# A float32r transformer trunk on one core: its on-chip pools laid out anew

## The chip, the cores and the metric

The kernel runs on one core of a Trainium2 chip. The metric is the device time of one execution in microseconds (us). Engines: PE (TensorE) multiplies matrices, DVE (VectorE), ACT (ScalarE) and POOL (GpSimd) work elementwise, SP (SyncE) issues the DMA transfers. SBUF is the on-chip memory of 128 partitions; an address here is a number of bytes within a partition. PSUM is the memory into which PE accumulates, in banks of 2 KiB a partition.

## The reference

Two layers, each of three blocks with a norm before and after, on x of 256 tokens by 1024:

```python
x = x + 0.5 * rms(swiglu(rms(x, g0), w_in[l,0], w_out[l,0]), g1)     # 1024 -> 2 x 2816 -> 1024
x = x + rms(mixer(rms(x, g2)), g3)
x = x + 0.5 * rms(swiglu(rms(x, g4), w_in[l,1], w_out[l,1]), g5)
```

`swiglu(h)` is `(silu(gate) * up) @ w_out` with `gate, up = split(h @ w_in)`. The mixer projects to 3080 columns: a differential attention of 4 heads (rotary embedding, two softmaxes, their difference on the values, a norm), and an mLSTM of 4 heads (a causal convolution of length 4 over queries and keys, exponential gates, a state carried over chunks of 64 tokens, an output gate). Both outputs, side by side, go through a matrix of 1024 by 1024. All is float32.

## The kernel before

Every product with a weight matrix is made of three float32r passes. An operand is split into hi and lo = value - hi, and `mm3` (L329 to L332) adds hi*hi (L330), hi*lo (L331) and lo*hi (L332) in one PSUM bank. The transposed activations are the stationary operand (128 x 128), the weights the moving one (128 x 512). There are 1312 such triples.

The tokens form two tiles of 128. The weights come as 164 pieces of 1 MiB in the order of use. SP loads a piece into one of three buffers `wr`. Each of its two halves is split by ACT, which writes hi into `wh` (L280), and by DVE, which writes lo into `wl` (L282); both are 4 KiB a partition. `wh` and `wl` have seven buffers each. The pool `k4` has six buffers that a mixer uses for its large tiles (`xpad`, `conv`, `gt`, `ex`, two of `qkT`, `vd`). While `lend` is set, which is everywhere but in the body of a mixer, each half whose running number ends in 2, 5 or 8 goes to two of these:

```python
if self.lend and self.halves % 10 in (2, 5, 8):
    lo = self.k4.tile([P, 1024], F32R, tag="k4", name=f"wl_{i}_{j}")
    hi = self.k4.tile([P, 1024], F32R, tag="k4", name=f"wh_{i}_{j}")
```

All buffers of a tag are as wide as its widest tile, padded to 32 bytes.

An FFN works through 11 chunks of 256 hidden columns. A chunk takes two pieces for its input products (PSUM tag `pin`, stationary tiles `th`, `tl` of the pool `tr`) and one for its output products (tag `bk`, stationary `hh`, `hl` of the pool `hp`). Between them stand silu on ACT, the product on DVE, two transposes per token tile (L461) and the split of the hidden layer into `hh` (L464) and `hl` (L465). The output products of a chunk run one or two chunks late; the last ones of the first token tile and then of the second end the FFN. The first chunk of the first FFN writes to `bk`.

A mixer's input projection runs as steps of one triple each (`part_step`), and its other stages are traced between them at positions given by hand (`AT`); the output projection has stationary tiles `yh`, `yl`, from the pool `tr` too, and the tag `bk`. `conv_input` takes `xpad` out of k4 and clears its first three columns on POOL (L788); ACT fills the rest (L795), ACT and DVE read it (L803, L806).

A planner with a simulated timeline sets the order on each engine from the traced order and the buffers that are free, apart from stretches where PE's order is that of the program text. Pools lie in SBUF in the order in which they are opened, from address 16512 on (a scratch ring of 16 KiB and small constants come first): `const`, `wr`, `wl`, `wh`, `tr`, `k2`, `k4`, `ded`, `hp`, `sm`.

Of the kernel before, what the change touches and what calls it, by code (L numbers as in the profile page):

```python
"""Two layers of macaron FFN / (diff attention | mLSTM) mixer / macaron FFN on one core.

Every product with a weight matrix runs as three float32r passes: an operand is
split exactly into hi (float32r, 12 significant bits) and lo = value - hi, and
hi*hi + hi*lo + lo*hi accumulate in one PSUM bank. The activations (transposed,
128 tokens a tile) are stationary and the weights move, 512 columns at a time.
"""
# [8 lines left out]
F32 = mybir.dt.float32  # L16
# [20 lines left out]
WARM = 6  # L37
PIECES_FFN = 3 * NC_FF
# [11 lines left out]
def _pack(inp):  # L50
    """Lays the inputs out for the kernel, in the order in which it uses them."""
# [67 lines left out]
class _Trunk:  # L119
# [49 lines left out]
    def constants_mix(self):  # L169
# [26 lines left out]
        # lambda of both layers, on every partition  # L196
# [8 lines left out]
        # persistent tiles with fixed parts  # L205
# [22 lines left out]
        nc.gpsimd.memset(self.vx, 1.0)  # L228

# [1 line left out]
    def after(self, ins, others):  # L231
        """ins takes its turn on its engine behind the others."""
        for o in others:
            self.tc.add_manual_dep(ins.ins, o.ins.name, mybir.DependencyInfo(
                mybir.DependencyClass.NoSync, mybir.DependencyReason.DATA), reason="turn")

    def table(self, name, last=None):
        """Loads a set of ScalarE's functions behind everything that uses another set."""
        self.loaded = self.nc.scalar.preload_act_table_set(name)
        self.after(self.loaded, self.users + ([last] if last else []))  # L240
        self.users = []

    def func(self, *args, **kw):
        """An activation that needs the set loaded last."""
        i = self.nc.scalar.activation(*args, **kw)  # L245
        self.after(i, [self.loaded])
        self.users.append(i)
        return i

    def piece(self):  # L250
        """The next 1 MiB of the weights as hi and lo: two times [P, 1024] each. While no
        mixer needs them, its 4 KiB buffers hold some of these."""
        parts = self.begin_piece()
        return [parts(), parts()]

    def begin_piece(self):
        """A function that gives a piece's halves one after the other."""
        nc, i = self.nc, self.piece_at
        self.piece_at += 1
        step = 1024  # L260
        if i in self.early:
            raw, step = self.early[i], 512
        else:
            raw = self.raw_tile(i)
            self.load = nc.sync.dma_start(raw.rearrange("p a b -> p (a b)"), self.a["w"][i])
        js = iter(range(2))

        def part():
            j = next(js)
# [3 lines that stand above are left out]
            else:  # L273
                lo = self.wl.tile([P, 1024], F32R, tag="wl", name=f"wl_{i}_{j}")
                hi = self.wh.tile([P, 1024], F32R, tag="wh", name=f"wh_{i}_{j}")
            self.halves += 1
            turns = self.turns.pop(0) if self.turns else ()
            for c in range(0, 1024, step):
                cs = slice(c, c + step)
                ia = nc.scalar.activation(hi[:, cs], raw[:, j, cs], AF.Copy)  # L280
                self.cast = ia
                iv = nc.vector.tensor_tensor(lo[:, cs], raw[:, j, cs], hi[:, cs].bitcast(F32), op=ALU.subtract)  # L282
                for oa, ov in turns:
                    self.after(ia, [oa] if oa else [])
                    self.after(iv, [ov] if ov else [])
            return hi, lo

        return part
# [4 lines left out]
    def start(self):  # L293
        """The first loads, in the order in which the products need them."""
# [20 lines left out]
    def warm(self, n):  # L315
        """The tensor engine's clock rises while it waits for the first loads."""
        bank = self.bank_bk()
        for _ in range(n):
            self.nc.tensor.matmul(bank, self.zero[:, 0:P], self.zero, start=True, stop=True)

    @staticmethod
    def cols(piece, k):
        """Columns k*512..k*512+511 of a piece, hi and lo."""
# [11 lines left out]
    def rsqrt(self, ss, width=1):  # L335
        """ss -> ss ** -0.5 on [P, width]."""
# [4 lines left out]
    def prenorm(self, t, gi):  # L341
        """Transposed x * gain of token tile t as hi/lo."""
        return [self.prenorm_half(t, gi, hf) for hf in range(2)]
# [19 lines left out]
    def square(self, t, hf, ss):  # L363
        """The mean square of half of token tile t."""
# [3 lines left out]
    def rstd(self, t):  # L368
        """rsqrt(mean(x ** 2) + eps) of token tile t."""
# [5 lines left out]
    def rsqrt_sum(self, ss, eps):  # L375
        """(ss0 + ss1 + eps) ** -0.5"""
# [9 lines left out]
    def postnorm(self, t, po, g, half):  # L386
        """x += (0.5 if half else 1) * rmsnorm(po) * g."""
# [83 lines left out]
    def ffn(self, pre, gi_post):  # L471
# [16 lines left out]
        if not xT:  # L488
            # the first phase: both token tiles from the start
# [41 lines left out]
        else:  # L531
            # the first two chunks: the first token tile runs ahead of the second
# [46 lines left out]
        # the last chunks: all of the first token tile, then the second  # L579
# [15 lines left out]
    def mixer(self, pre, gi_post):  # L595
# [19 lines left out]
        # output projection  # L615
# [24 lines left out]
    def lambdas(self):  # L640
        """-(exp(q1.k1) - exp(q2.k2) + lambda_init) of both layers, on every partition."""
# [8 lines left out]
class _Mixer:  # L650
    """The stages of one layer's mixer, in the order in which they are traced."""
# [13 lines left out]
    def traverse(self, tr, pin, ws, pins1, ws1, load_gpost):  # L665
        """The rest of the input projection in steps of three matrix products, with everything
        else that the mixer does between them."""
# [53 lines left out]
    def stages(self):  # L721
        """(step, stage): the stage takes its turn once so many steps of the products are traced."""
# [37 lines left out]
    def part(self, t, kh, pin, w):  # L760
        """Half the contraction of one token tile with one group of 512 columns."""
# [7 lines left out]
    def transposed(self, a, tag="ptr"):  # L769
        """The four 128-column blocks of a, transposed, in a PSUM bank."""  # L770
# [12 lines left out]
    # ---- queries and keys of the mLSTM  # L783
    def conv_input(self, t, pin):
        tr = self.tr
        if t == 0:
            self.xpad = tr.t4("xpad", (P, 4, S + 3))
            tr.nc.gpsimd.memset(self.xpad[:, :, 0:3], 0.0)  # L788
# [26 lines left out]
    # ---- gates of the mLSTM  # L815
# [13 lines left out]
    def gate_inputs(self):  # L829
        """log i and the forget gate's input, tokens on partitions."""  # L830
# [24 lines left out]
    def gate_rows(self):  # L855
        """Cumulative log forget gates b, u = log i - b and the running maxima, heads on
        partitions 0..3, 32..35, 64..67 and 96..99."""
# [34 lines left out]
    def gate_exps(self, t):  # L892
        """exp(u_s - M_j) within a chunk and s <= j, zero elsewhere: one contraction over both."""
# [9 lines left out]
    def gate_decays(self):  # L903
        """The decays, input weights and exp(-m)."""
# [8 lines left out]
        # the first chunk's state is zero: its queries meet it with a factor of zero  # L913
# [5 lines left out]
    def weighted_qk(self):  # L919
        """Queries times their decay, keys times their input weight."""  # L920
# [24 lines left out]
    def intra_weights(self):  # L945
        """exp(u_s - M_j) * (k_s . q_j) / 8. Heads on other partitions use another PSUM bank."""
# [13 lines left out]
    # ---- attention  # L960
# [15 lines left out]
    def roped(self, i, t, scale):  # L976
        """Queries (i = 0) or keys (i = 1), transposed."""
# [10 lines left out]
    def scores(self, t, h0):  # L988
        """Both softmaxes of some heads before the division: exp(s - max) and its sums."""
# [29 lines left out]
    def combine(self, t, h0):  # L1019
        """l0 * (p0 - lambda * p1), transposed: [key, head, query]."""  # L1020
# [37 lines left out]
    # ---- state and output of the mLSTM; column 128 of a head's values is one, for the denominator  # L1058
# [36 lines left out]
    def output_gate(self, pin, t):  # L1095
        """tanh(o / 2): sigmoid(o) is half of it plus one."""
# [9 lines left out]
    def normed_ml(self, t):  # L1106
        """rmsnorm(num / max(|den|, exp(-m))) but for its gain: the norm takes the division's place."""
# [18 lines left out]
    def outputs_ml(self, t):  # L1126
        """sigmoid(o) times the normed output, transposed."""
# [4 lines left out]
def _trunk(tc, a, out, phases=3 * L):  # L1132
    nc = tc.nc
    with contextlib.ExitStack() as st:
        def pool(name, bufs, **kw):
            return st.enter_context(tc.tile_pool(name=name, bufs=bufs, **kw))
        pools = (pool("const", 1), pool("wr", 3), pool("wl", 7), pool("wh", 7), pool("tr", 6), pool("k2", 10), pool("k4", 6),
                 pool("ded", 1), pool("hp", 4), pool("sm", 2), pool("ps", 1, space=PSUM))
# [26 lines left out]
```

## Time and profile before

| | us |
|---|---|
| median of 3 runs | 1016.41 |
| lowest and highest | 1015.97 and 1016.7 |
| span of the profiled execution | 1012.0 |
| median above that span | 4.4 |

The profile is of one execution. Its span runs from the first instruction of the program to the last; the time of a run also has what lies before and behind it, so sums over the trace stand against the span. The profiled execution's whole time is not listed apart from its span; the runs put it at 4.0 to 4.7 us above. Of the engines in the span, the profile gives busy time; of matmuls, which overlap, the duration up to a modelled end. The pace of a stream of matmuls is read from starts.

### The profile page before, as it was taken

How to read it: one execution, taken by the hardware profiler on the slowest of the kernel's cores; microseconds unless marked ns; L12 is line 12 of the kernel's file. 1: busy time of each engine (PE TensorE's matmuls, PEld its weight loads, DVE VectorE, ACT ScalarE, POOL GpSimd, SP SyncE). 2: the span in 40 equal slices, each digit the busy share in tenths (PEclk: the TensorE clock that was granted, in tenths of full speed). 3: DMA queues.
4: the chain of work that ended last, by engine and by line, in shares of the span. 5: the costliest groups of instructions: out<-in, count | busy, mean ns of one | idle time of the engine just before them, and what ended most of it. 6: DMA issues, size and time to landing. Idle time of an engine off the chain costs nothing.

```text
span 1012.0 us, 12195 instructions
## 1 busy us (share of the span) xinstructions
PE 997.7 (99%) x4701; PEld 807.3 (80%) x4701; DVE 616.0 (61%) x867; ACT 523.5 (52%) x853; POOL 58.3 (6%) x60
## 2 busy tenths in 40 slices
PE   8999999999999999999999999999999999999997
PEld 5888888887788888888888888888877888888885
DVE  6755454589766755555485545456988586454542
ACT  6644444466755654444375544445768465444431
POOL 2000000014010000000000000001230100000000
PEclk9999999999999999999999999999999999999999
DMA  7954545335352745454346455543554247554511
GB/s 276 353 206 151 197 172 191 131 125 186 132 202 84 279 158 208 166 214 191 136 177 260 152 188 201 191 148 119 179 176 140 110 163 274 185 190 166 206 45 42
DMA packets 26809, 178.86 MB, mean 177 GB/s; under 512 B 2970, under 2 KB 3354, under 8 KB 6014
## 3 DMA queue, kind: packets, MB, share of 16 engines
q1 hardware_dynamic: 26750, 178.07, 48.4%
q8 instruction: 37, 0.61, 0.2%
q14 instruction: 22, 0.18, 0.1%
HBM read 177.01 MB, written 1.05 MB: 176 GB/s over the span
## 4 chain that ended last, share of the span: by engine, by line
PE 92%; DVE 5%; ACT 1%; DMA 1%; issue 0%; SPq 0%; DVEq 0%; POOLq 0%; ACTq 0%
PE pin L330 19%; PE pin L332 18%; PE pin L331 18%; PE bk L330 10%; PE bk L332 10%; PE bk L331 10%; PE ptr L461 2%; DVE wl L282 2%; DVE conv L806 1%; PE ptr L349 1%; PE ptr L773 1%; DMA wr<-in_w_dram 1%; ACT p L245 1%; PE bk L1086 1%; PE bk L1041 1%; ACT wh L280 0%
## 5 line engine op out<-in xcount | busy, mean ns | idle before, releaser
L282 DVE TENSOR_TENSOR wl<-wr,wh 128x1024 fp32r<-128x1024 f32 (+1 forms) x332 | 397.6, 1219 | 229.2 <-ACT wh L280 225.8
L280 ACT ACTIVATE wh<-wr 128x1024 fp32r<-128x1024 f32 (+1 forms) x332 | 340.4, 1045 | 203.5 <-PE pin L332 110.9
L330 PE MATMUL pin<-wh,th 128*128 128x512 f32 x880 | 350.7, 399 | 0.6 <-DVE rb L972 0.6
L332 PE MATMUL pin<-wh,tl 128*128 128x512 f32 x880 | 344.8, 392 | 0.0
L331 PE MATMUL pin<-wl,th 128*128 128x512 f32 x880 | 344.7, 392 | 0.0
L332 PEld LDWEIGHTS pin<-wh,tl 128*128 128x128 f32 x880 | 165.2, 188 | 36.4
L330 PEld LDWEIGHTS pin<-wh,th 128*128 128x128 f32 x880 | 165.3, 188 | 35.8 <-issue 1.0
L331 PEld LDWEIGHTS pin<-wl,th 128*128 128x128 f32 x880 | 165.5, 188 | 33.3
L330 PE MATMUL bk<-wh,hh 128*128 128x512 f32 x352 | 141.5, 402 | 0.0
L331 PE MATMUL bk<-wl,hh 128*128 128x512 f32 x352 | 139.6, 396 | 0.0
L332 PE MATMUL bk<-wh,hl 128*128 128x512 f32 x352 | 139.3, 397 | 0.0
L464 ACT ACTIVATE hh<-ptr 128x256 fp32r<-128x256 f32 x88 | 33.2, 378 | 101.2 <-PE ptr L461 83.3
L245 ACT ACTIVATE sil<-pin,rs 128x256 f32<-128x256 f32 x86 | 40.7, 473 | 75.3 <-PE pin L332 70.6
L332 PEld LDWEIGHTS bk<-wh,hl 128*128 128x128 f32 x352 | 66.2, 188 | 15.2
L331 PEld LDWEIGHTS bk<-wl,hh 128*128 128x128 f32 x352 | 66.2, 188 | 14.4
L330 PEld LDWEIGHTS bk<-wh,hh 128*128 128x128 f32 x352 | 66.2, 188 | 14.5
L465 DVE TENSOR_TENSOR hl<-ptr,hh 128x256 fp32r<-128x256 f32 x88 | 37.1, 422 | 59.2 <-ACT hh L464 56.3
L454 DVE SCALAR_TENSOR_TENSOR h<-pin,rs,sil 128x256 f32<-128x256 f32 x86 | 41.3, 480 | 31.9 <-ACT sil L245 31.9
L338 POOL TENSOR_TENSOR rs<-s,c_half 128x1 f32<-128x1 f32 x24 | 18.3, 766 | 623.1 <-DVE s L378 613.3
L461 PEld LDWEIGHTS ptr<-c,h 128*128 128x128 f32 x176 | 24.6, 140 | 11.9
L395 DVE TENSOR_TENSOR tmp<-bk,gpost 128x512 f32<-128x512 f32 x24 | 16.3, 689 | 29.3 <-ACT junk L392 29.3
L461 PE MATMUL ptr<-c,h 128*128 128x128 f32 x176 | 33.5, 272 | 0.0
(169 smaller groups left out, 617.0 us busy)
## 6 DMA issues: line engine op xcount, KB each, us to landing
wr<-in_w_dram SPq DMA_DIRECT2D x162, 1024.0 KB, 4.8
gpost<-in_gpost_dram SPq DMA_DIRECT2D x6, 512.0 KB, 6.4
wr<-in_w_dram SPq DMA_DIRECT2D x3, 512.0 KB, 8.9
x<-in_x_dram SPq DMA_DIRECT2D x4, 256.0 KB, 7.0
out_dram<-x SPq DMA_DIRECT2D x4, 256.0 KB, 2.0
wr<-in_w_dram SPq DMA_DIRECT2D x2, 256.0 KB, 4.6
lamv<-in_lam_dram SPq DMA_DIRECT2D x1, 256.0 KB, 3.2
c<-in_c_dram SPq DMA_DIRECT2D x1, 222.0 KB, 6.7
```

Source lines behind the costliest of these rows:

```text
L245: i = self.nc.scalar.activation(*args, **kw)
L280: ia = nc.scalar.activation(hi[:, cs], raw[:, j, cs], AF.Copy)
L282: iv = nc.vector.tensor_tensor(lo[:, cs], raw[:, j, cs], hi[:, cs].bitcast(F32), op=ALU.subtract)
L330: mm(ps, xh, wh, start=start, stop=False)
L331: mm(ps, xh, wl, start=False, stop=False)
L332: mm(ps, xl, wh, start=False, stop=stop)
L338: self.nc.gpsimd.tensor_tensor(r, ss, self.half[:, :width], op=ALU.pow)
L395: nc.vector.tensor_tensor(tmp[hf], po[hf], g[:, hf * 512:hf * 512 + 512], op=ALU.mult)
L454: nc.vector.scalar_tensor_tensor(h, pin[:, 256:512], r, sil, op0=ALU.mult, op1=ALU.mult)
L461: nc.tensor.transpose(ptr[:, k, :], h[:, k * P:(k + 1) * P], self.ident)
L464: nc.scalar.activation(hh, ptr, AF.Copy)
L465: nc.vector.tensor_tensor(hl, ptr, hh.bitcast(F32), op=ALU.subtract)
```

## The change

Nothing is computed differently. The scratch ring at address 0, which serves DMAs issued by POOL, shrinks from 16 KiB to 1 KiB. A filler of 896 bytes brings the first pool to address 2048. The pools are opened in another order, so that those of the weights, the activations and the lent tiles (`wr`, `wl`, `wh`, `tr`, `k4`) start at multiples of 2 KiB, and behind them `hp` and `k2`; a second filler in `const` does the same for `ded`. `xpad` (4 x 259 float32 a partition, 4144 bytes) becomes one buffer of `ded`, allocated and cleared once, so the widest tile of k4 is 4096 bytes. Docstrings and comments become empty lines. The core of the diff:

```diff
+SCRATCH = 1024
+FILL = 896
+CFILL = 384
...
         nc.gpsimd.memset(self.vx, 1.0)
+        self.xpad = self.ded.tile([P, 4, S + 3], F32, name="xpad")
+        nc.gpsimd.memset(self.xpad[:, :, 0:3], 0.0)
...
         if t == 0:
-            self.xpad = tr.t4("xpad", (P, 4, S + 3))
-            tr.nc.gpsimd.memset(self.xpad[:, :, 0:3], 0.0)
+            self.xpad = tr.xpad
...
-        pools = (pool("const", 1), pool("wr", 3), pool("wl", 7), pool("wh", 7), pool("tr", 6), pool("k2", 10), pool("k4", 6),
-                 pool("ded", 1), pool("hp", 4), pool("sm", 2), pool("ps", 1, space=PSUM))
+
+        fill = pool("fill", 1)
+        fill.tile([P, FILL // 4], F32, name="fill")
+        wr, wl, wh, trp, k4 = pool("wr", 3), pool("wl", 7), pool("wh", 7), pool("tr", 6), pool("k4", 6)
+        hp, k2, const, ded = pool("hp", 4), pool("k2", 10), pool("const", 1), pool("ded", 1)
+        const.tile([P, CFILL // 4], F32, name="cfill")
+        pools = (const, wr, wl, wh, trp, k2, k4, ded, hp, pool("sm", 2), pool("ps", 1, space=PSUM))
...
-    nc = bacc.Bacc("TRN2", target_bir_lowering=False, num_devices=1)
+    nc = bacc.Bacc("TRN2", target_bir_lowering=False, num_devices=1, dynamic_dma_scratch_size=SCRATCH)
```

## Rows read from the trace of the kernel before

**Rows 1.** The page: span, and busy us (share) and instructions of each engine.
```profile
span 1012.0 us, 12195 instructions
...
PE 997.7 (99%) x4701; PEld 807.3 (80%) x4701; DVE 616.0 (61%) x867; ACT 523.5 (52%) x853; POOL 58.3 (6%) x60
```

**Rows 2.** The page: shares of the chain that ended last, by engine.
```profile
PE 92%; DVE 5%; ACT 1%; DMA 1%; issue 0%; SPq 0%; DVEq 0%; POOLq 0%; ACTq 0%
```

**Rows 3.** Three stretches: us, busy us (instructions) by engine, clock, DMA share, GB/s.
```profile
186.30:197.00 10.70, 10.70 (x47) 8.64 (x46) 3.64 (x7) 1.76 (x5) 0.68 (x2) 1.00 0.40 165
249.30:255.00 5.70, 5.70 (x27) 4.73 (x26) 3.93 (x5) 3.07 (x4) 0.00 (x0) 1.00 0.72 263
330.00:494.00 164.00, 164.00 (x733) 133.24 (x732) 92.25 (x105) 79.46 (x104) 0.00 (x0) 1.00 0.54 197
```

**Rows 4.** Timeline of PE in the first mixer: start, duration, engine, line; starts counted between.
```profile
247.38 0.39 PE L331 MATMUL pin<-wl,th 128*128 128x512 f32 x1
...
249.23 0.39 PE L330 MATMUL pin<-wh,th 128*128 128x512 f32 x1
...
250.13 0.39 PE L331 MATMUL pin<-wl,th 128*128 128x512 f32 x1
...
254.90 0.39 PE L331 MATMUL pin<-wl,th 128*128 128x512 f32 x1
```

**Rows 5.** Timeline of PE, first and last of 47 products at the first FFN's end.
```profile
186.30 0.40 PE L331 MATMUL bk<-wl,hh 128*128 128x512 f32 x1
...
197.00 0.39 PE L332 MATMUL bk<-wh,hl 128*128 128x512 f32 x1
```

**Rows 6.** The page's groups: line, engine, form, count; busy us, mean ns; idle before.
```profile
L282 DVE TENSOR_TENSOR wl<-wr,wh 128x1024 fp32r<-128x1024 f32 (+1 forms) x332 | 397.6, 1219 | 229.2 <-ACT wh L280 225.8
...
L332 PE MATMUL pin<-wh,tl 128*128 128x512 f32 x880 | 344.8, 392 | 0.0
L331 PE MATMUL pin<-wl,th 128*128 128x512 f32 x880 | 344.7, 392 | 0.0
...
L331 PE MATMUL bk<-wl,hh 128*128 128x512 f32 x352 | 139.6, 396 | 0.0
L332 PE MATMUL bk<-wh,hl 128*128 128x512 f32 x352 | 139.3, 397 | 0.0
```

**Rows 7.** Groups of PE from 284 to 313 us (a mixer's end).
```profile
L331 PE MATMUL bk<-wl,yh 128*128 128x512 f32 x24 | 9.4, 391 | 0.0
...
L331 PE MATMUL pin<-wl,th 128*128 128x512 f32 x10 | 3.9, 390 | 0.0
```

**Rows 8.** Groups of PE from 249 to 255.1 us.
```profile
L331 PE MATMUL pin<-wl,th 128*128 128x512 f32 x10 | 3.9, 389 | 0.0
```

**Rows 9.** Timeline of PE around half 175 (third FFN, chunk 2).
```profile
542.57 0.39 PE L330 MATMUL pin<-wh,th 128*128 128x512 f32 x1
...
543.25 0.40 PE L330 MATMUL pin<-wh,th 128*128 128x512 f32 x1
...
546.72 0.39 PE L330 MATMUL pin<-wh,th 128*128 128x512 f32 x1
...
548.77 0.39 PE L330 MATMUL pin<-wh,th 128*128 128x512 f32 x1
```

**Rows 10.** Timeline of PE around half 182 (third FFN, chunk 3).
```profile
558.17 0.39 PE L330 MATMUL pin<-wh,th 128*128 128x512 f32 x1
...
559.54 0.39 PE L330 MATMUL pin<-wh,th 128*128 128x512 f32 x1
```

**Rows 11.** Line L282: duration ns min/median/max, first and last start, forms.
```profile
L282 DVE TENSOR_TENSOR wl<-wr,wh x332: 681/1225/2311, 5.7 to 978.0; 128x1024 fp32r<-128x1024 f32 x162, 128x512 fp32r<-128x512 f32 x4
```

**Rows 12.** Tile xpad: duration ns min/median/max, first and last start, forms.
```profile
L795 ACT ACTIVATE xpad<-ptr x4: 577/590/602, 211.9 to 728.0; 128x512 f32<-128x512 f32 x4
L788 POOL MEMSET xpad<- x2: 109/111/113, 196.5 to 680.1; 128x12 f32 x2
```

**Rows 13.** The page's DMA queues: packets, MB, share of 16 engines.
```profile
q1 hardware_dynamic: 26750, 178.07, 48.4%
```

## The prediction

> **What bounds the kernel now.** I read the page first [rows 1]: the execution spans 1012.0 us and PE is busy for 99% of it. The chain that ended last gives 92% of the span to PE, 5% to DVE and 1% each to ACT and DMA [rows 2]. In the FFN stretch from 330 to 494 us, PE is busy for all 164.00 us, in 733 matmuls [rows 3]; DVE and ACT have slack there and so do the transfers. A ns off each matmul of an FFN is therefore a ns off the end, and only in the mixers do other engines sometimes set the pace.
>
> Busy time says nothing about the pace of matmuls that overlap, so I went on to the timeline and divided the distance between two starts by the matmuls between them. Matmuls of one shape (128x128 stationary, 128x512 moving) show several paces:
> - 226.8 ns in a quiet stretch of the mixer: 249.23 to 254.90 us, 25 steps, 5.67 us [rows 4].
> - 232.6 ns at the end of the first FFN, in products of the hidden layer (stationary hh, hl): 186.30 to 197.00 us, 46 steps, 10.70 us, without a break [rows 5].
> - 229.2 ns over the 12 steps from 247.38 to 250.13 us, soon after transposes interrupted the stream; the last of them already run at 226.8 [rows 4].
>
> The groups say the same of the whole execution. L331 and L332 take 392 ns from start to modelled end on th, tl, and 396 to 397 on hh, hl [rows 6]. In the fast stretch it is 389 [rows 8]. The durations follow the paces, so a difference in duration can stand for one in pace.
>
> What makes hh slower? Not the other engines: in the slow stretch DVE is busy 34% and ACT 16% of the time and DMA has a share of 0.40; in the fast one it is 69%, 54% and 0.72, at a granted clock of 1.00 in both [rows 3]. Not the PSUM tag: yh, yl products write the same tag bk and take 391 ns [rows 7]. What is left is where the operand lies. The trace holds no addresses; those of the program follow from the pools' sizes in the order in which they open, with tiles padded to 32 bytes. wl, wh, tr start 1792 bytes past a multiple of 2 KiB, a multiple of 256. The buffers of hh and hl come behind vx (4128 bytes) and start 32 bytes past a multiple of 64. The k4 slots are as wide as their widest tile, xpad: 4 x 259 x 4 = 4144, padded to 4160. So the six slots start at 1792, 1856, 1920, 1984, 0 and 64 past a multiple of 2 KiB; four of them at no multiple of 256.
>
> The k4 slots hold lent weights. Half n of a piece (n = 2 x piece + half) is lent when n ends in 2, 5 or 8. Half 175 is read by the six products from 543.25 us on. Before it the pace is 226.7 (0.68 us for 3). From 543.25 to 546.72 it is 231.3 (3.47 us for 15), although the last 9 of these read halves 176 and 177, which lie in wl and wh; then 227.8 (2.05 us for 9) [rows 9]. So an operand at an odd place costs a few ns, and the stream needs some nine products to settle again.
>
> **The change part by part.**
> - *hp at multiples of 1 KiB.* hh and hl get the residues that th and tl have modulo 256. There are 352 x 3 = 1056 such products [rows 6]. If they go to the settled pace: 232.6 - 226.8 = 5.8 ns, or 6.1 us. If all are as in the 12 steps after a break: 232.6 - 229.2 = 3.4 ns, 3.6 us. By durations (396 and 397 against yh's 391) it is 5 to 6 ns. An FFN chunk runs its 24 output products behind or between transposes, so some settling remains; I take 5 ns: **5.3 us**, between 3.6 and 6.3.
> - *k4 slots at multiples of 2 KiB,* which needs xpad to leave (4160 would become 4096). Pin products of FFNs: 2640 in all [rows 6] less 2 x 288 of the mixers, which read unlent halves, is 2064. Their mean is near 392 ns; in the mixer stretch with lending off L331 takes 390 [rows 7], settled products 389 [rows 8]. Between 0 (if breaks alone unsettle them) and 3 ns, or 6.2 us. By that event, 15 x (231.3 - 226.8) = 68 ns for a lent half [rows 9]; the four FFNs have 4 x 66 halves, 3 in 10 are lent and 2 in 3 of these feed pin products, 53 in all: 3.6 us. As some fall into a stretch that a break has unsettled anyway, I take **3.5 us**.
> - *wl, wh, tr, k2, wr* move from 1792 to 0 past 2 KiB and keep their residues modulo 256 and their distances from each other. Slot five, already at a multiple of 2 KiB, holds the hi part of half 182: 6 products in 1.37 us, 228.3 ns each, with a wl partner at an odd place [rows 10]. No gain or loss beyond the above shows there: 0, between the bounds of the rivals.
> - *Casts* into these buffers: on DVE 1225 ns median over buffers of all residues, and a mean of 1219 that is not above it, so no kind of buffer stands out [rows 6, 11]; ACT's are shorter still. 0; if they changed, PE hides them in the FFNs.
> - *xpad of its own.* One memset on POOL (111 ns) in the first FFN, where POOL is nearly idle, in place of two at the mixers' heads [rows 12]. The first stood at 196.5 us, 15 us ahead of ACT's first write into xpad at 211.9; nobody waited for it, and without that cover it would cost its 0.1 us. Layer 1's writes now follow layer 0's reads of the one buffer, some 490 us earlier. k4 has one tenant less in a mixer (six tiles in six slots instead of seven), which can only free slots sooner. xpad now lies 32 past 64; its readers are on DVE and ACT, for which the casts show no price. 0, with up to 0.5 us either way, because the planner may order the mixer's work differently.
> - *Scratch ring 1 KiB.* Every transfer of the kernel goes through the hardware queue [rows 13]; none is issued by POOL. 0. *Fills and docstrings*: no instruction.
>
> Sum: 5.3 + 3.5 = 8.8 us of the 1012.0 us span. What lies outside the span (the median of the runs is 1016.41, 4.4 us above it) stays. **1016.4 - 8.8 = 1007.6 us.**
>
> **The rivals.**
> *Place does not matter; same time.* The slow products could be slow for another reason that goes with hh, such as h having just come from the transposes. For it: no row ties a pace to an address, only the program's layout does. Against: the 47 products from 186.30 us on run long after their transposes and stay slow. Then 1016.4. [...]
>
> *Slower: a common start.* With everything at a multiple of 2 KiB, the moving half and the stationary tile of k = 0 begin at one residue, and both are read at once. If the products on th, tl (2640, and some 240 of the output projection and the first chunk) fell from the 229.2 of the unsettled stream to hh's 232.6 ns, that is +9.8 us; with hh no better, 1026.2. It decides against the gain of 8.8 us from 3.1 ns a product on. Against it: before, wh and th also share one residue (1792) and run at 226.8 [rows 4].
>
> *More: everything settles.* If the breaks unsettle the stream only because odd places keep it so: 6.3 + 6.2 = 12.5 us, 1003.9. Against: the stream also needs settling after a break with no odd place near [rows 4].
>
> **How the numbers follow.** The forecast has 0.70, with its own range from 1003.9 to 1012.8 (3.6 us for hh, nothing for lending); everything settles 0.10; no change 0.11; slower 0.09. A difference of 0.2%, 2 us, is about what measurement can tell here: faster 0.80, same 0.11, slower 0.09. The range runs from 1003.0 to 1015.0: it leaves out the slower case, part of no change and a little below the best case.
>
> **What would show it.** Right: hh, hl products of L331 and L332 at 390 to 393 ns instead of 396 to 397; the 47 products at the end of an FFN at 227 to 228 ns a step; pin products at 390 to 391; the mixers' length nearly unchanged, since their products are already well placed; chain and waits as before. Wrong: hh still at 396 (place does not matter), th, tl above 392 (a common start), or the gain in the matmuls taken back by new waits of PE on casts in the mixers.

## The result and the profile after

The changed kernel takes 1004.63 us (median of 4 runs, 1004.17 to 1006.06), the kernel before, beside it, 1016.19 (4 runs, 1014.46 to 1016.7). The ratio is 0.9896, with a 95% interval of 0.9885 to 0.9908: 11.6 us less. The two profiled spans are 9.6 us apart, 1012.0 and 1002.4. PE, ACT, DVE and SP each carry out the same instructions in the same order; POOL has one memset of `xpad` less. Line numbers are up by 4 or 5 (`mm3` is L335 to L337, formerly L330 to L332; the transposes of x L354, formerly L349).

The page of the kernel after: span, busy time by engine, shares of the chain, and the groups that answer to [rows 6].

```profile
span 1002.4 us, 12193 instructions
PE 987.8 (99%) x4701; PEld 807.1 (81%) x4701; DVE 615.6 (61%) x867; ACT 523.6 (52%) x853; POOL 57.9 (6%) x59
PE 93%; DVE 4%; ACT 1%; DMA 1%; issue 0%; SPq 0%; DVEq 0%; POOLq 0%; ACTq 0%
...
L287 DVE TENSOR_TENSOR wl<-wr,wh 128x1024 fp32r<-128x1024 f32 (+1 forms) x332 | 397.3, 1218 | 227.0 <-ACT wh L285 217.3
L337 PE MATMUL pin<-wh,tl 128*128 128x512 f32 x880 | 343.9, 391 | 0.0
L336 PE MATMUL pin<-wl,th 128*128 128x512 f32 x880 | 343.4, 390 | 0.0
L337 PE MATMUL bk<-wh,hl 128*128 128x512 f32 x352 | 137.9, 393 | 0.0
L336 PE MATMUL bk<-wl,hh 128*128 128x512 f32 x352 | 137.6, 391 | 0.0
```

Products on hh, hl fell from 396 and 397 ns to 391 and 393, those on th, tl from 392 to 390 and 391 [rows 6]. The casts did not move (1219 and 1218 ns). PE is as full as it was, 99%: it does the same work at a quicker pace.

The timeline of PE after shows that pace: first and last of the products at the first FFN's end, and a stretch of the third FFN in which pin products are followed by output products (start, duration).

```profile
183.98 0.39 PE L336 MATMUL bk<-wl,hh 128*128 128x512 f32 x1
...
194.43 0.39 PE L337 MATMUL bk<-wh,hl 128*128 128x512 f32 x1
...
539.00 0.39 PE L335 MATMUL pin<-wh,th 128*128 128x512 f32 x1
...
543.09 0.39 PE L335 MATMUL pin<-wh,th 128*128 128x512 f32 x1
...
545.80 0.39 PE L335 MATMUL bk<-wh,hh 128*128 128x512 f32 x1
```

183.98 to 194.43 us is 46 steps in 10.45 us, 227.2 ns each; before it was 232.6 [rows 5]. From 539.00 to 545.80 lie 30 steps in 6.80 us, 226.7 ns, the pace of the quiet mixer stretch before [rows 4], right across the passage from th to hh at 543.76.

The chain gives landmarks: each handover between an FFN and a mixer, or between two FFNs, begins with eight transposes of x. Of the kernel before:

```profile
197.40 0.87 PE ptr L349 x8
...
325.13 0.87 PE ptr L349 x8
...
505.50 0.87 PE ptr L349 x8
514.73 0.87 PE ptr L349 x8
694.70 0.87 PE ptr L349 x8
...
822.30 0.87 PE ptr L349 x8
```

And of the kernel after:

```profile
194.82 0.87 PE ptr L354 x8
...
322.18 0.87 PE ptr L354 x8
...
500.28 0.87 PE ptr L354 x8
509.35 0.87 PE ptr L354 x8
687.40 0.88 PE ptr L354 x8
...
814.78 0.87 PE ptr L354 x8
```

| stretch | before, us | after, us | change |
|---|---|---|---|
| first FFN, from its first product (9.05 and 9.00) | 188.35 | 185.82 | -2.53 |
| first mixer with both handovers | 127.73 | 127.36 | -0.37 |
| second FFN | 180.37 | 178.10 | -2.27 |
| handover between the layers | 9.23 | 9.07 | -0.16 |
| third FFN | 179.97 | 178.05 | -1.92 |
| second mixer with both handovers | 127.60 | 127.38 | -0.22 |
| fourth FFN, to the end of the span | 189.70 | 187.62 | -2.08 |

The four FFNs give 8.80 us, all else 0.80. The first row holds the start of the program, which does not repeat: it is 188.12 us in a second profile of the kernel before, and 185.68 to 186.99 in those of kernels whose products lie as after's do. Counted from PE's 61st matmul (some 20 us in) the first FFN takes 177.17 us in both profiles of the kernel before and 174.84 after, 2.33 less; the four FFNs then give 8.60. In the stretch from 330 to 494 us PE now gets through 743 matmuls, as against 733 [rows 3].

### The profile page after: what moved, and what is told of

Read it like the earlier page. It is cut to its first block, busy times and chain, and to the rows that moved or that the text cites. A ratio compares the mean times of both kernels' runs of the same rounds, so it can differ in the third digit from the quotient of the medians.

```text
span 1002.4 us, 12193 instructions
## 1 busy us (share of the span) xinstructions
PE 987.8 (99%) x4701; PEld 807.1 (81%) x4701; DVE 615.6 (61%) x867; ACT 523.6 (52%) x853; POOL 57.9 (6%) x59
## 4 chain that ended last, share of the span: by engine, by line
PE 93%; DVE 4%; ACT 1%; DMA 1%; issue 0%; SPq 0%; DVEq 0%; POOLq 0%; ACTq 0%
PE pin L335 19%; PE pin L337 19%; PE pin L336 19%; PE bk L335 10%; PE bk L337 10%; PE bk L336 10%; PE ptr L466 2%; DVE wl L287 2%; DVE conv L810 1%; PE ptr L354 1%; ACT p L250 1%; PE ptr L778 1%; DMA wr<-in_w_dram 1%; PE bk L1090 1%; PE bk L1045 1%; ACT wh L285 0%
## 5 line engine op out<-in xcount | busy, mean ns | idle before, releaser
L287 DVE TENSOR_TENSOR wl<-wr,wh 128x1024 fp32r<-128x1024 f32 (+1 forms) x332 | 397.3, 1218 | 227.0 <-ACT wh L285 217.3
L335 PE MATMUL pin<-wh,th 128*128 128x512 f32 x880 | 349.2, 397 | 0.6 <-DVE rb L976 0.6
L337 PE MATMUL pin<-wh,tl 128*128 128x512 f32 x880 | 343.9, 391 | 0.0
L336 PE MATMUL pin<-wl,th 128*128 128x512 f32 x880 | 343.4, 390 | 0.0
L337 PEld LDWEIGHTS pin<-wh,tl 128*128 128x128 f32 x880 | 165.2, 188 | 35.0
L335 PEld LDWEIGHTS pin<-wh,th 128*128 128x128 f32 x880 | 165.3, 188 | 34.5 <-PE ptr L778 1.0
L336 PEld LDWEIGHTS pin<-wl,th 128*128 128x128 f32 x880 | 165.5, 188 | 32.4
L335 PE MATMUL bk<-wh,hh 128*128 128x512 f32 x352 | 140.0, 398 | 0.0
L337 PE MATMUL bk<-wh,hl 128*128 128x512 f32 x352 | 137.9, 393 | 0.0
L336 PE MATMUL bk<-wl,hh 128*128 128x512 f32 x352 | 137.6, 391 | 0.0
L337 PEld LDWEIGHTS bk<-wh,hl 128*128 128x128 f32 x352 | 66.1, 188 | 13.7
L336 PEld LDWEIGHTS bk<-wl,hh 128*128 128x128 f32 x352 | 66.2, 188 | 12.7
L335 PEld LDWEIGHTS bk<-wh,hh 128*128 128x128 f32 x352 | 66.1, 188 | 12.8
```

The lines of the kernel that those rows point to most:

```text
L335: mm(ps, xh, wh, start=start, stop=False)
L336: mm(ps, xh, wl, start=False, stop=False)
L337: mm(ps, xl, wh, start=False, stop=stop)
```

## The experiments

The theory: a product runs at 226.7 ns a step only when its moving operand (the weights) and its stationary operand (the activations) start at the same place modulo some power of two, and a product that does not unsettles the stream for those behind it. The rivals: the absolute place of each buffer counts; another part of the change counts (ring, order of the pools, multiples of 2 KiB, xpad); place does not matter. Residues below are modulo 256 unless said; after the change wl, wh, tr, k4 and hp all have residue 0. FFN stretches below are the second and third, read from the chain as above: before 180.37 + 179.97 = 360.34 us, after 356.15. These two stretches repeat to some 0.02 us where the layout is unchanged, so they measure more finely than the medians.

### The kernel before again

> The kernel before once more, unchanged. It shows how far one execution lies from another and what lies around the span. If the profiled execution of before was only a quick one, spans of about 1012 to 1015 us stand here with 1.8 us around them, as with the changed kernel (1004.17 us for a span of 1002.4). If the larger scratch ring costs time outside the span, the time is about 4.4 us above the span. Ratio to the kernel before 1.000 either way.

Median 1015.31 (10 runs, 1013.42 to 1017.3), ratio 0.9999 [0.9988, 1.0011]; FFN stretches 360.34 again. A mixer was longer in its profile, which the last section takes up.

### The hidden layer moved by 32

Against after; a second pool keeps what follows in its place.

```diff
+        pa = pool("pa", 1)
+        pa.tile([P, 32 // 4], F32, name="pa")
         hp = pool("hp", 4)
+        pb = pool("pb", 1)
+        pb.tile([P, 2016 // 4], F32, name="pb")
```

> The changed kernel with hp alone moved by 32 bytes (32 past a multiple of 1 KiB), everything behind it back at its place. Theory (the address of the stationary tile sets the pace): hh, hl products fall back to 233 ns a step and 396 to 397 ns on L336 and L337, pin products after them are unsettled a little longer; 1056 times 5.2 ns, 5.5 us: 1010. Rival (the gain is that of everything starting at multiples of 2 KiB, or of the lent slots alone): hh stays at 391 to 393 ns and the time at 1004.6.

Median 1009.8 (1008.19 to 1010.6), ratio 0.9937 [0.9922, 0.9952]: 5.2 us above after. FFN stretches 179.22 + 179.18 = 358.40, by these rows of the chain:

```profile
324.85 0.88 PE ptr L354 x8
...
504.07 0.87 PE ptr L354 x8
513.19 0.87 PE ptr L354 x8
692.37 0.87 PE ptr L354 x8
```

The page's groups:

```profile
L336 PE MATMUL pin<-wl,th 128*128 128x512 f32 x880 | 343.4, 390 | 0.0
...
L336 PE MATMUL bk<-wl,hh 128*128 128x512 f32 x352 | 139.4, 396 | 0.0
```

Only hh is slow again. The same instructions, in the same order, on the same data, lose 5.2 us for 32 bytes in the place of one pool, so place does matter, and this is what hh costs on its own at a distance of 32. In the kernel before, hp starts 160 past a multiple of 256 by the program's addresses, a distance that no run takes by itself.

### Lent slots 4160 bytes apart

Against after: the slots are as wide as before the change (the tile `conv` is made wider, and a filler of 1664 bytes behind k4 keeps the rest in place), so four of six have residues 64, 128, 192 and 64.

```diff
-            self.conved = tr.t4("conv", (P, 4, S))
+            self.conved = tr.t4("conv", (P, 4, S + 3))[:, :, 0:S]
```

> The changed kernel with the six k4 slots 4160 bytes apart again (they start at 0, 64, 128, 192, 0 and 64 modulo 256), hp and all the rest at multiples of 2 KiB as before this edit. Theory (lent weights at odd places cost 2 to 4 ns a product and unsettle those after them): pin products of FFNs at 229.5 instead of 227.7 ns, 3.5 to 4 us, and a little for the lent halves in output products: 1008.5 to 1009. With e1 it makes up the whole difference. Rival (only stationary tiles matter): 1004.6.

Median 1013.16 (10 runs, 1010.2 to 1015.26), ratio 0.9976 [0.9965, 0.9988]: 8.5 us above after, well above what was expected. FFN stretches 179.44 + 179.52 = 358.96:

```profile
324.74 0.87 PE ptr L354 x8
...
504.18 0.87 PE ptr L354 x8
513.36 0.87 PE ptr L354 x8
692.88 0.87 PE ptr L354 x8
```

The page's groups:

```profile
L336 PE MATMUL pin<-wl,th 128*128 128x512 f32 x880 | 345.2, 392 | 0.0
...
L336 PE MATMUL bk<-wl,hh 128*128 128x512 f32 x352 | 138.3, 393 | 0.0
```

hp lies well here, and yet hh takes 393 instead of 391: lent halves also feed output products, and unsettle those behind them. PE's order is the same in every run, so its starts can be laid against after's product by product. Of the 2.81 us that the two FFNs lose, 0.96 fall on products that read a lent tile off the residue and 1.82 on the twelve products behind each of these; all others together lose 0.04. By the stretches the cost is (358.96 - 356.15) x 2 = 5.6 us in four FFNs. In the profiled execution the handovers lose another 0.7 us, and a longer second mixer 1.7, as in the repeat of the kernel before.

### All lent slots moved by 64

A filler of 64 bytes before `k4` and one of 1984 behind it, as for `hp` above; the slots stay at equal residues, all of them 64.

> The changed kernel with the six k4 slots 4096 bytes apart but all 64 past a multiple of 2 KiB: lent weights lie at one odd residue instead of four. If what unsettles the stream is a step from one moving residue to another, the cost of the steps into and out of lent halves stays: 1008 to 1012. If it is the four different residues among the slots, or the slots at 128 and 192, 1005 to 1006.

Median 1014.54 (10 runs, 1012.95 to 1016.34), ratio 0.9992 [0.9983, 1.0002]; the FFN stretches are 179.97 + 180.08 = 360.05, by these rows of the chain:

```profile
326.99 0.87 PE ptr L354 x8
...
506.96 0.87 PE ptr L354 x8
516.17 0.87 PE ptr L354 x8
696.25 0.87 PE ptr L354 x8
```

The expectations were too low. It is not that the slots differ among themselves: with six slots of six off the residue of tr and hp the loss in the two FFNs is 3.90 us, with four of six 2.81, a ratio of 1.39 where 6 to 4 would give 1.5. Two FFNs have 132 halves, 40 of them lent, so a lent half off the residue costs 98 ns. Each is read twice, by six products for either token tile (`in_piece` and `out_part` run once for each tile), so that one reading costs 49 ns; the 68 of the prediction was one reading of one half [rows 9]. Nearly the whole gain of the change is gone, by the place of three halves in ten.

### The activations of tr moved by 32

Fillers of 32 bytes before and 2016 behind `tr`.

> The changed kernel with tr alone moved by 32 bytes: the stationary tiles th, tl, yh, yl lie 32 past a multiple of 512, all moving operands at multiples of 2 KiB, hh and hl too. Theory (32 past a multiple of 64 costs a stationary tile 6 ns a product): 2880 products at 233 instead of 227.8 ns, 15 us: 1019.5; and hh, hl stay at 228. Rival (the tag bk, the transposes or the hidden layer make hh slow): 1004.6.

Median 1019.75 (1018.99 to 1020.84), ratio 1.0043 [1.0027, 1.0058], slower than before the change. FFN stretches 361.82. The page's groups:

```profile
L336 PE MATMUL pin<-wl,th 128*128 128x512 f32 x880 | 348.7, 396 | 0.0
...
L336 PE MATMUL bk<-wl,hh 128*128 128x512 f32 x352 | 138.0, 392 | 0.0
```

Now th, tl are slow and hh is not. The slow kind follows the place of the stationary tile, not the operand's name, its history or its PSUM tag.

### Everything moved: by 256, by 64

`FILL = 896 + 256` puts none of these pools at a multiple of 2 KiB, `FILL = 896 + 64` none at a multiple of 128; they still share one residue.

> The changed kernel with 256 bytes more of filler, so that every pool starts 256 past a multiple of 2 KiB and each 2 KiB moving operand crosses a 2 KiB boundary. Theory (what counts is the residue modulo 256 or less): no change, 1004.6, settled pace 226.7 ns. Rival (multiples of 2 KiB count): part of the gain is lost, above 1007.

> The changed kernel with 64 bytes more of filler: every pool moves by 64 and all operands of the products share the residue 64 modulo 256. Theory A (operands must share one residue): settled pace 226.7 ns, 1004.6. Theory B (they must start at multiples of 256): the pace settles at 228.7 ns or not at all, 2 ns on 3936 products, 8 us: 1012 or more.

By 256: 1005.18 (1004.05 to 1005.69), ratio 0.9892 [0.9877, 0.9907]. By 64: 1005.27 (1005.12 to 1005.77), ratio 0.9901 [0.9884, 0.9917]. FFN stretches 356.15 and 356.14. The groups of the kernel moved by 64:

```profile
L336 PE MATMUL pin<-wl,th 128*128 128x512 f32 x880 | 343.7, 391 | 0.0
...
L336 PE MATMUL bk<-wl,hh 128*128 128x512 f32 x352 | 137.8, 391 | 0.0
```

Both keep the whole gain: in these moves the absolute place does not count, and the multiples of 2 KiB do nothing by themselves.

### The hidden layer moved by 64, 128 and 256

As for 32, with 64, 128 and 256 in its place (and 1984, 1920 and 1792 behind). They ask modulo what the residue counts.

> The changed kernel with hp moved by 64 instead of 32 bytes. If a stationary tile needs a multiple of 64: as the changed kernel, 1004.6, hh at 228 ns. If it needs 128 or more, or the residue of the moving operand: 1007 to 1010, hh at 230 to 233 ns.

> The changed kernel with hp moved by 128 bytes. The runs so far say that moving and stationary operand must share a residue (all at 64: 226.7 ns; stationary alone moved by 32 or 64: 233 ns). If the residue counts modulo 128 or less: as the changed kernel, 1004.6, hh, hl at 228 ns. If modulo 256: hh, hl at 233 ns, 1010.

> The changed kernel with hp moved by 256 bytes. If the residue counts modulo 256 or less: 1004.6, hh, hl at 228 ns. If modulo 512 (all tiles of tr lie 512 bytes apart, so no run has told these apart yet): hh, hl at 233 ns, 1010.

| hp moved by | median, us | ratio [95%] | FFN stretches, us |
|---|---|---|---|
| 32 | 1009.8 | 0.9937 [0.9922, 0.9952] | 358.40 |
| 64 | 1011.63 (5 runs) | 0.9963 [0.995, 0.9976] | 358.94 |
| 128 | 1010.46 | 0.9949 [0.9931, 0.9966] | 358.39 |
| 256 | 1004.89 | 0.9888 [0.9867, 0.991] | 356.14 |

The group of hh at 128 and at 256:

```profile
L336 PE MATMUL bk<-wl,hh 128*128 128x512 f32 x352 | 139.3, 396 | 0.0
```

```profile
L336 PE MATMUL bk<-wl,hh 128*128 128x512 f32 x352 | 137.6, 391 | 0.0
```

At a distance of 256 the products settle; at 128, 64 and 32 they don't. Of the distances tried, the multiples of 256 are the good ones.

### The constants at residue 0

`CFILL = 256` in place of 384 brings x and the identity of the transposes to residue 0, where h already was, to see whether transposes gain too.

> The changed kernel with the filler in const 256 instead of 384 bytes: x and the identity matrix lie at multiples of 256 instead of 128 past one, so that the 176 transposes of the hidden layer have a moving identity at the residue of their stationary h. If transposes follow the same rule as the products: up to 6 ns off each of 176 transposes and less settling behind the some 140 breaks (27 ns each now), 1 to 4 us: 1001 to 1004, faster than both kernels. If breaks and transposes do not care: 1004.6.

Median 1004.91 (1004.06 to 1005.76), ratio 0.9892 [0.9874, 0.991]: not faster than after. The FFN stretches are 355.73, 0.42 us less for two FFNs, which the medians can't show. As a way to beat the kernel after it missed.

### Two edits to the kernel before

If shared residues are all that counts, two edits to the kernel before must give the whole gain: `conv` made 4352 = 17 x 256 bytes wide, so that the slots of k4 stay at one residue, and 224 bytes put into `ded` so that hp starts at a multiple of 256. The ring stays at 16 KiB, the pools in their old order at 1792 past 2 KiB, and xpad in k4.

```diff
+        self.ded.tile([P, 224 // 4], F32, name="pad")
...
-            self.conved = tr.t4("conv", (P, 4, S))
+            self.conved = tr.t4("conv", (P, 4, 272))[:, :, 0:S]
```

> The kernel before with two edits and nothing else of the change: conv, a tile of k4, is made 4352 bytes wide (17 times 256), and 224 bytes are put behind wt, so that hp starts at a multiple of 256. The ring stays 16 KiB, xpad stays in k4, the pools stay in their order and at 1792 past 2 KiB. If one residue modulo 256 for all operands of the products is all that the change gives: settled pace 226.7 ns, 1004.6. If the ring, the order of the pools, xpad's own buffer or the multiples of 2 KiB have a part in it: between 1006 and 1016.

Median 1004.77 (1004.15 to 1005.53), ratio 0.9895 [0.9879, 0.9912], as after. The page's groups, and two rows of its chain (the second FFN's ends):

```profile
L332 PE MATMUL pin<-wl,th 128*128 128x512 f32 x880 | 343.4, 390 | 0.0
...
L332 PE MATMUL bk<-wl,hh 128*128 128x512 f32 x352 | 137.6, 391 | 0.0
```

```profile
322.20 0.87 PE ptr L350 x8
...
500.30 0.87 PE ptr L350 x8
```

178.10 us, the second FFN of the kernel after to the last digit. The other parts of the change have no share in the gain.

## Why the prediction was right, and where it was off

Forecast were 1007.6 us, faster than before, in a range from 1003.0 to 1015.0; 1004.63 were measured.

**The bound.** PE's pace in the FFNs sets the end: the FFNs gave 8.80 of the 9.60 us between the spans, and the instructions, their order and the shares of the chain stayed as they were.

**hh and hl, 5.3 us.** Right in kind, and somewhat large: 5.2 us by the medians when hp alone was moved by 32. By the FFN stretches it is (358.40 - 356.15) x 2 = 4.5 us, or 4.3 ns for each of 1056 products, where the prediction took 5. Laid against after product by product, the kernel before loses 4.19 us in the two FFNs, 2.33 of them on hh and hl and 1.83 on th and tl: 4.7 and 3.7 us in four. The 47 products run at 227.2 ns, as foretold.

**Lent halves, 3.5 us.** The mechanism was right; the size came near with a wrong price and a wrong count. The term counted the 53 lent halves that feed pin products at 68 ns, and left out the 27 that feed output products. That holds only while hh is slow anyway: putting the lent slots right with hp still off is worth (360.34 - 358.40) x 2 = 3.9 us, close to the 3.5. But the 68 ns belong to one reading of half 175, from 543.25 us on, for the second token tile. The first tile's products had read it before, from 539.58 us:

```profile
539.58 0.40 PE L330 MATMUL pin<-wh,th 128*128 128x512 f32 x1
...
540.95 0.40 PE L330 MATMUL pin<-wh,th 128*128 128x512 f32 x1
```

Two readings for each of 53 halves at 68 ns would have been 7.2 us. A reading costs less on the whole: by the 3.9 us it is 37 ns for each of 106. Half 175 has both its tiles off the residue by the program's addresses, as only 28 of the 80 lent halves do, and its second reading fell into a settled stream (226.7 ns a step ahead of it [rows 9]). That the price was nearly twice too high where the count was half of what it should be is luck. With hp right, the lent slots cost 5.6 us by the stretches, 70 ns for each of all 80 lent halves, 35 for a reading. Likewise hh is worth only (360.34 - 358.96) x 2 = 2.8 us while the lent slots are off. The two terms are not independent, since a lent half off the residue unsettles well-placed products behind it: each alone, they give 2.8 and 3.9, and both together (360.34 - 356.15) x 2 = 8.4. These differences set hp at 32 beside hp at 160, and lent tiles beside lent tiles in other slots, since xpad has left their turn; with hp at 64 in place of 32, the loss in four FFNs is 1.1 us larger. The prediction's sum of 8.8 came out because its lent term was read beside slow hh and its hh term beside settled products; that the FFNs as a whole stand at 8.80 to the digit is chance, with 8.60 in what repeats and errors of 0.2 to 0.8 us, of opposite sign, in the two terms.

**What the sum left out.** The handovers gave 0.67 us and the mixers and the start 0.13: products of the last and first chunks run there too. Then the frame. The prediction laid the sum from 1016.4 and put 4.4 us outside the span. In every run of this case the time is 1.73 to 1.84 us above its span (1004.17 and 1002.4 for after's profile, 1016.25 and 1014.5 for the repeat of before), so before's profiled execution took some 1013.8 us and was a quick one, and the 4.0 to 4.7 us given with the profile before are not what lies around a span. From the profiled executions the difference is 9.6, from the medians 11.6 (1016.19 - 1004.63). A larger count lies between: 57 executions of the layout before have a mean of 1015.5 us, 24 of the six kernels with shared residues (after, all by 256, all by 64, hp by 256, the constants, two edits) 1005.0. Of these 10.5 us the stretches explain 9.6, or 9.35 without the start, which does not repeat.

**The zeros.** Ring, order of the pools, multiples of 2 KiB, xpad and casts at nothing: right, shown by the two edits (1004.77) and the move by 256 (1005.18); the casts' mean is unchanged.

**Why odd places are slow.** The prediction spoke of odd places, of "32 past a multiple of 64" and "no multiple of 256". It was the wrong wording of the right thing: with every pool 64 past, nothing is lost, and with hp alone 64 past, the loss is no smaller than at 32. What counts is whether the two operands of a product share their residue modulo 256: with hp 128 off, L336 takes 396 ns on hh, with hp 256 off 391. By the layout of before the prediction could not tell the two apart, since wl, wh and tr shared theirs. Which part of the chip causes it, no run here shows; the last section has a hint.

**The rivals.** "Place does not matter" fell with the moves of hp and of tr alone: with hp moved by 32 bytes L336 takes 396 ns in place of 391 on hh, with tr moved by 32 bytes 396 in place of 390 on th. "A common start" fell with after itself: both operands start at one residue and th, tl take 390, not more. "Everything settles" gave 1003.9, and the median lies nearer to it than to 1007.6, but not by its mechanism: it asks 12.5 us of the FFNs, and they gave 8.6 to 8.8; the stream is still unsettled behind transposes. From 330 to 494 us of the kernel after, the second to tenth step behind them takes 230.7 ns on the mean, the eleventh to the 29th 226.5 to 226.8, and L336 stands at 390 and 391 instead of 389 [rows 8].

## What to carry to other kernels

All of this was seen with float32r matmuls of one shape (128x128 by 128x512). Where a stream of them has PE full and two groups of one shape differ by a few ns, work out where their operands start, and give moving and stationary buffers one residue modulo 256 bytes: make tiles that set a tag's width multiples of 256, and put a filler ahead of a pool that follows odd-sized ones. Read pace from starts over long stretches, and compare layouts by stretches between landmarks of the chain, away from the start: the two FFNs used here repeat to 0.02 us where the median of some runs moves by 1. Price such parts together, each with the other undone and with it done, since what one of them unsettles lands on the products of the other.

## What the runs showed of the hardware that was not expected

That place counts only as a distance, modulo 256 bytes, is told above. The starts, read in ns, also show where the delay begins. With hp moved by 32, a settled stream on th passes to hh 36 times, and the first slow step is not that of the first product on hh but that of the last on th: 235 ns, with 226 or 227 before it. In the kernel before, with hp at 160, that step is 236 ns on the mean of 20 such passes from 325 to 690 us; in the kernel after it is 226. Where the moving operand leaves the residue instead, with all lent slots moved by 64, the last product before a lent half still takes 226 to 228 ns, and the first on it 235 to 237, in all 24 such places. With hp moved by 32 the weight load of a product starts as the product before it does: that of a first product on hh at 547.56 us, with the last product on th, while the product itself follows at 547.79. So what has to agree may be the moving operand of a product and the stationary tile that is loaded meanwhile, that of the next; it fits every such place, but no run was made to test it.

Besides, the granted clock differed. In the repeat of before the second mixer, from the landmark at 705.68 to that at 812.88 us, took 107.2 us and not 105.6, and the windows (us, busy us and instructions of PE, PEld, DVE, ACT and POOL, then the granted clock, DMA share and GB/s) show where:

```profile
773.00:774.00 1.00, 1.00 (x6) 0.76 (x6) 1.00 (x2) 1.00 (x3) 0.00 (x0) 1.00 0.00 0
774.00:775.00 1.00, 1.00 (x5) 0.71 (x5) 0.98 (x2) 1.00 (x4) 0.00 (x0) 0.71 0.50 66
775.00:776.00 1.00, 1.00 (x4) 0.81 (x3) 1.00 (x1) 0.69 (x4) 0.00 (x0) 0.50 0.66 221
776.00:777.00 1.00, 1.00 (x3) 0.78 (x3) 0.03 (x1) 1.00 (x2) 0.00 (x0) 0.50 1.00 426
777.00:778.00 1.00, 1.00 (x4) 0.78 (x3) 0.75 (x1) 0.86 (x7) 0.00 (x0) 0.59 0.86 352
778.00:779.00 1.00, 1.00 (x10) 0.59 (x10) 0.48 (x1) 0.00 (x0) 0.00 (x0) 1.00 0.00 0
```

The granted clock goes from 1.00 to 0.50 and comes back; by the means of these windows it was at 0.50 for 3.4 us. In the us ahead of the fall PE started six matmuls and was busy throughout. The same stretch in before's first profile has as few, six, six and five in the three us from 771 to 774, also with PE busy throughout, at a clock of 1.00. The kernel with lent slots 4160 apart shows such a fall too (0.72, 0.50, 0.50 and 0.57 in the four us from 771 to 775, a mixer of 107.3 us). The mean granted clock of an execution, which every run lists, is 0.994 or lower in 25 of the 57 executions of the layout before, in 7 of 20 with lent slots off, in 4 of 13 with hp off, and in none of the 24 with shared residues; with tr off it is 0.995 in all 4. The means over the 57 and the 24 are 0.9953 and 0.9967. That would be 1.4 us of a span if all time went with the clock, but it does not: a straight line through the 81 times, with one slope for both layouts, gives 0.3 us less for each 0.001 more of clock, so 0.4 us for this difference, and 10.1 us between the layouts at an equal clock. So the clock holds about half of the 0.9 us that the stretches leave open, as an estimate, and the rest is not explained. Why the layout should bear on the clock is not settled; part of these differences lies at the start. There the clock of the first 16 us is 0.89 in both profiles of the kernel before and in that of the kernel after, and 1.00 with the lent slots 4160 apart. In that one, too, the products from 9.53 to 11.23 us start 0.42 or 0.43 us apart, as those from 9.59 to 11.30 us in the kernel after, so a clock of 1.00 in the windows need not mean that PE ran at the full pace.
